# Mean squares of the attention heads: summed over the partitions by GpSimd in place of TensorE

## The chip, the core and the metric

The kernel runs on one core of a Trainium2 chip. A core has a matrix engine (TensorE, PE in the profile; its weight loads are PEld), three engines that work on 128 partitions side by side (VectorE or DVE, ScalarE or ACT, GpSimd or POOL), queues that issue transfers (SP and ACT here), an on-chip memory of 128 partitions (SBUF) and accumulators for TensorE (PSUM, in banks of 512 float32 columns). Each engine takes its instructions in order, and engines wait for one another on semaphores. The metric is the device time of one execution in microseconds.

## What is computed

A block of two layers over 272 tokens (16 learned ones and 256 of input), width 1024. Each layer has a mixer of three branches (retention with 4 heads, a gated recurrence with 8, differential attention with 8) and a feed-forward part with a short convolution. What matters here: each head's output is divided by its own root mean square.

```python
def _rms(x):
    xf = x.astype(F32)
    return xf * lax.rsqrt(jnp.mean(xf * xf, axis=-1, keepdims=True) + EPS)
...
    o = _rms(from_chunks(o)) * jax.nn.silu(gate)                          # retention, 256 values a head
...
    o = _rms(from_chunks(o)) * jax.nn.silu(gate)                          # gated recurrence, 128 values a head
...
    o = _rms(o) * subln_g.astype(F32) * (1.0 - lambda_init)               # differential attention, 128 values a head
```

## The kernel before

Activations are held transposed: features on the 128 partitions, the tokens (272, in the second layer 258) along the free dimension. A mean over a head's 128 values is thus a sum over partitions.

The main work is products of weights with activations. To keep float32 precision each operand is split into a rounded high part and a low rest, and each 128x128 weight tile is used by three matmuls (`products`, lines 915 to 917: high by high, high by low, low by high). Weights come from HBM in chunks of eight tiles, 512 KB (`_Weights.next`): a transfer to `wraw` (three buffers), ScalarE rounds it to `whi`, VectorE subtracts to `wlo` (four buffers each). The order of the products is written out in `ORDER`; a name with `+` there starts a job that runs behind the products: `hg_heads`, `hg_outputs` (gated recurrence, four heads at a time), `ret_head` (retention), `da_heads` (differential attention, two heads at a time), `da_tail` (the tokens that do not fill a block).

No engine's order is written by hand. Every operation is recorded with a cost, a due time (`plan.key`) and the tiles that it touches; `_Plan.order` then runs a list schedule and fixes the order in which all engines get their instructions. A cost is a fixed part plus a part per column (`_Engine.__getattr__`, line 571 on; for GpSimd's arithmetic 0.04 us + (0.85e-3 + 1.6e-3) us per column). A handoff to another engine is booked at 0.4 us (`CROSS`), a buffer's return at 0.5 us (`FREE`). As all helpers record through one line, most instructions bear L593 in the profile, so they are told apart by their tiles.

A head's end, before the change: its output `o` (tiles `ro`, `ho`, `do`) lies in a PSUM bank of the pool "acc", which has two. `mean` squares the upper and the lower 64 partitions on ScalarE into `hsq` and `hso`, adds them on VectorE, rounds the sum on ScalarE into the upper half of `hsh`, puts the rest beside it on VectorE, and TensorE sums the 128 rows of `hsh` with a matrix of 1/128 into a PSUM bank `ms`, so that every partition holds the mean. `rsqrt` takes Ln and Exp of it on ScalarE (`hr`), and VectorE multiplies `o` by `hr`. For retention the squares of the head's two halves have been added before, and `mean` gets them as they are. `da_tail` calls it (through `sub_norm`) once for a group of four heads, with 128 columns. The norm over a token's 1024 features (`Norm.finish`) uses `mean` as well, three times; its scaled activations `y` are made on GpSimd.

Of the kernel before, what the change touches and what calls it, by code (L numbers as in the profile page):

```python
# [12 lines left out]
F32R = mybir.dt.float32r  # L13
U8 = mybir.dt.uint8
AF = mybir.ActivationFunctionType
# [4 lines left out]
P = 128  # L20
# [3 lines left out]
T = META + SEQ  # L24
D = 1024
# [532 lines left out]
class _Engine:  # L558
# [5 lines left out]
    def __getattr__(self, method):  # L564
        f = getattr(self.engine, method)

        def call(*args, **kw):
            aps = [(k, x) for k, x in list(enumerate(args)) + list(kw.items()) if isinstance(x, bass.AP)]
            outs = [x for k, x in aps if k in (0, "out", "accum_out")]
            ins = [x for k, x in aps if k not in (0, "out", "accum_out")]  # L570
            n = math.prod(outs[0].shape[1:])
            cost = self.fixed + self.each * n
            if self.name == "act":
                cost += 0.093 * (len(aps) - 2) - (0.043 if ins[0].tensor.name in self.plan.psum else 0.0)
            elif self.name == "pool" and method != "memset":
                cost += 1.6e-3 * n
            if method == "scalar_tensor_tensor":
                cost += 0.06
            if method == "reciprocal":
                cost += 7 * self.each * n  # L580
            elif method == "tensor_tensor_scan":
                cost += self.each * n
            elif method == "transpose":
                cost = 0.11
            elif method == "matmul" and args[1].dtype == F32R:
                cost = max(0.107, n / 2400 + 0.003)
            elif method == "matmul":
                cost = max(0.214 if args[1].shape[-1] > 32 else 0.07, 4 * n / 2400)
            elif method == "dma_start":
                cost = self.fixed + self.each * n * outs[0].shape[0]  # L590

            count = self.name == "pe" and (2 if method == "transpose" or args[1].dtype == F32R else 4)
            self.plan.add(self.name, lambda: f(*args, **kw), cost, outs, ins, args[2] if method == "activation" else None, count)  # L593

        return call
# [56 lines left out]
def _trace(ctx, tc, plan, a, depth, probe):  # L652
    nc = tc.nc
    act = _Engine(plan, nc.scalar, "act", 0.094, 0.833e-3)
    dve = _Engine(plan, nc.vector, "dve", 0.068, 1.042e-3)
    pe = _Engine(plan, nc.tensor, "pe", 0.0, 4 / 2400)
    pool = _Engine(plan, nc.gpsimd, "pool", 0.04, 0.85e-3)
# [7 lines left out]
    tp = ctx.enter_context(tc.tile_pool(name="tp", bufs=2))  # L665
# [6 lines left out]
    def new(pool_, shape, dt, tag, bufs, name):  # L672
        serial[0] += 1
        return plan.tile(pool_, shape, dt, tag, bufs, f"{name}_{serial[0]}")

    def fixed(shape, name, dt=F32):
        return new(cp, shape, dt, name, 1, name)
# [10 lines left out]
    def temp(cols, tag, bufs=2):  # L688
        return new(tp, [P, cols], F32, tag, bufs, tag)
# [55 lines left out]
    def ones_round(value, name):  # L745
        t = fixed([P, P], name, F32R)
        f = slot("ones")[:, :P]
        pool.memset(f, value)
        act.activation(t, f, AF.Copy)
        return t  # L750
# [8 lines left out]
    ones_h = ones_round(1.0 / 128, "ones_h")  # L759
# [11 lines left out]
    rstd = fixed([P, T], "rstd")  # L771
# [37 lines left out]
    def rsqrt(out, ms, scale=1.0):  # L809

        act.activation(out, ms, AF.Ln, bias=eps, scale=scale)
        act.activation(out, out, AF.Exp, scale=-0.5)

    class Norm:
# [34 lines left out]
        def finish(self):  # L849
            if self.rest is None:  # L850
                self.halves()
            else:
                tt(self.sum, self.sum, self.rest, ADD)
            if self.apart:
                rsqrt(rstd[:, self.first :], mean(ones_h, self.sum, AF.Copy), P / D)
            else:

                ps = bank("ms")[:, self.first : T]
                pe.matmul(ps, ones_d, self.sum, start=True, stop=True)
                rsqrt(rstd[:, self.first :], ps)  # L860
# [106 lines left out]

    top, low = slice(0, P // 2), slice(P // 2, P)

    def mean(ones_, x, func):  # L970


        n = x.shape[1]
        sums = x[top] if func == AF.Copy else temp(T, "hsq")[top, :n]
        other = temp(T, "hso", 1)[top, :n]
        act.activation(other, x[low], func)
        if func != AF.Copy:
            act.activation(sums, x[top], func)
        tt(sums, sums, other, ADD)
        both = new(tp, [P, T], F32R, "hsh", 2, "hsh")[:, :n]  # L980
        act.activation(both[top], sums, AF.Copy)
        dve.tensor_tensor(out=both[low], in0=sums, in1=both[top].bitcast(F32), op=SUB)
        ms = bank("ms")[:, :n]
        pe.matmul(ms, ones_, both, start=True, stop=True)
        return ms

    def split_blocks(name, blocks, t0):

# [8 lines left out]
    for li in range(depth):  # L997
# [4 lines left out]
        t0 = T0 if last else 0  # L1002
# [29 lines left out]
        def ret_head(hd):  # L1032
            q, k, vt, gate = st["rq"], st["rk"], st["rvt"], st["rg"]
            if hd == 0:
                st["dec"] = slot4("dec")
                sync.dma_start(st["dec"].rearrange("p h t -> p (h t)"), a["dec"])
            dec = st["dec"][:, hd, :]

            s1 = bank("s1")
            a1 = temp(T + P + TAIL, "wts")  # L1040
            parts = ((0, t0, t0, dec[:, t0:]), (P, P, T, dec[:, : P + TAIL]))
            for k0, q0, at, _ in parts:
                pe.matmul(s1[:, at : at + T - q0], k[:, hd, k0 : k0 + P], q[:, hd, q0:], start=True, stop=True)
                plan.hold(a1)
            for _, q0, at, by in parts:
                tt(a1[:, at : at + T - q0], s1[:, at : at + T - q0], by, MUL)
            os = [acc_bank("ro") for _ in range(2)]
            sq = temp2("sum", 1)
            for e in range(2):
                o = os[e]  # L1050
                ec = slice((hd * 2 + e) % 4 * P, (hd * 2 + e) % 4 * P + P)
                v = vt[(hd * 2 + e) // 4]
                pe.matmul(o[:, t0:T], v[:, 0, ec], a1[:, t0:T], start=True, stop=False)
                pe.matmul(o[:, P:T], v[:, 1, ec], a1[:, T : T + P + TAIL], start=False, stop=True)
            for e in range(2):
                i = (e * 4 + hd) * TAIL
                tt(os[e][:, 2 * P : T], os[e][:, 2 * P : T], st["ro"][:, i : i + TAIL], ADD)
            for e in range(2):
                act.activation(sq[:, e, t0:], os[e][:, t0:T], AF.Square)
            tt(sq[:, 0, t0:], sq[:, 0, t0:], sq[:, 1, t0:], ADD)  # L1060
            r = temp(T, "hr")
            rsqrt(r[:, t0:], mean(ones_h, sq[:, 0, t0:], AF.Copy), 0.5)
            for e in range(2):
                g = gate[:, hd * 2 + e, t0:]
                y = temp(T, "ho")[:, t0:]
                tt(y, os[e][:, t0:T], r[:, t0:], MUL)
                tt(g, y, g, MUL)
# [242 lines left out]
        def hg_outputs(b, am, at, ax):  # L1310
            vt = st[f"hvt{b}"]
            pt = bank("ht")[:, : 4 * TAIL]
            pe.matmul(pt, st[f"hvs{b}"], am, start=True, stop=True)
            inside = temp(4 * TAIL, "am", 3)
            act.activation(inside, pt, AF.Copy)
            for hd in range(4):
                g = st["hg"][:, 4 * b + hd, t0:]
                o = acc_bank("ho")
                ec = slice(hd * P, hd * P + P)
                pe.matmul(o[:, t0:P], vt[:, 0, ec], at[:, hd, t0:P], start=True, stop=False)  # L1320
                pe.matmul(o[:, P:T], vt[:, 0, ec], ax[:, hd, :], start=False, stop=False)
                pe.matmul(o[:, P:T], vt[:, 1, ec], at[:, hd, P:], start=False, stop=True)
                tt(o[:, 2 * P : T], o[:, 2 * P : T], inside[:, hd * TAIL : (hd + 1) * TAIL], ADD)
                r = temp(T, "hr")
                rsqrt(r[:, t0:], mean(ones_h, o[:, t0:T], AF.Square))
                y = temp(T, "ho")[:, t0:]
                tt(y, o[:, t0:T], r[:, t0:], MUL)
                tt(g, y, g, MUL)
# [97 lines left out]
        def sub_norm(out, o):  # L1426
            n = o.shape[1]
            r = temp(T, "hr")[:, :n]
            rsqrt(r, mean(ones_h, o, AF.Square))
            stt(out, o, subg[:, li : li + 1], r, MUL, MUL)  # L1430

        def da_tail(b):
# [111 lines left out]
        for name, j in ORDER:  # L1544
# [18 lines left out]
            elif name[0] == "*":  # L1563
                plan.key = clock[0] - MARGIN
                n = name[1:]
# [9 lines left out]
            both = slice(2 * j, 2 * j + 2)  # L1575
            if name in BASE:
# [32 lines left out]
                elif name in ("hi", "dv"):  # L1609
                    n = name[0] + "v"  # L1610
# [115 lines left out]
```

## Time and profile before

| | |
|---|---|
| time, median of 3 runs | 1301.69 us (1301.66 to 1302.56) |
| span of the profiled execution, first to last instruction | 1299.9 us |
| matmuls, busy | 10965, 1290.8 us |
| VectorE, busy | 993.4 us |
| ScalarE, busy | 855.9 us |
| GpSimd, busy | 85.6 us, 162 instructions |
| granted TensorE clock, mean | 0.999 |
| read from HBM | 216.19 MB |

A row of the groups gives line, engine, operation, the tile written and the tiles read, shape and count, then busy time in us and the mean in ns, then the engine's idle time just before them and who ended it. A row of the waits gives who waited for whom: total us, times, longest. A row of a tile's view gives the count and the shortest, median and longest duration in ns, then the first and last start in us and the shapes. A row of the timeline gives start and duration in us. A row of the stretches gives busy time and instruction count of each engine between two times. Records of matmuls overlap, so the time that one takes is read from the spacing of their starts, or from a stretch in which TensorE is always busy.

### The profile page before, as it was taken

What the parts mean: (1) busy time and instruction counts of PE and PEld (TensorE: products, weight loads), DVE (VectorE), ACT (ScalarE), POOL (GpSimd) and SP (SyncE); (2) the same over time, 40 slices, a digit from 0 to 9 for tenths busy, and PEclk for the clock granted to TensorE, in tenths of its full rate; (3) what the DMA queues carried; (4) which work ended last, traced back from release to release, by engine and by line L of the source; (5) the groups of instructions that cost most, each with busy time, mean ns of one, the idle gap of its engine ahead of it and who ended that gap; (6) DMA issues with size and microseconds to landing.
All of it is one profiled execution on the core that took longest, in us unless ns stands there. A gap on an engine that the chain in (4) does not pass through costs nothing.

```text
span 1299.9 us, 27225 instructions
## 1 busy us (share of the span) xinstructions
PE 1290.8 (99%) x10965; PEld 1268.7 (98%) x10965; DVE 993.4 (76%) x1745; ACT 855.9 (66%) x1490; POOL 85.6 (7%) x162
## 2 busy tenths in 40 slices
PE   9999999999999999999999999999999999999998
PEld 8999999999999999999999999999999999999986
DVE  7685888698686789886565868886997868899753
ACT  6765565766777568776456664657667876787743
POOL 5000000000100020000020000000001100200000
PEclk9999999999999999999999999999999999999999
DMA  8555444435544555555555455454444456556653
GB/s 279 195 159 155 167 149 154 146 136 158 162 143 152 180 161 184 187 173 170 178 179 181 161 171 171 146 172 140 149 161 163 146 163 197 173 186 202 201 183 109
DMA packets 60751, 219.01 MB, mean 168 GB/s; under 512 B 6864, under 2 KB 6992, under 8 KB 60624
## 3 DMA queue, kind: packets, MB, share of 16 engines
q1 hardware_dynamic: 60336, 216.74, 51.6%
q8 instruction: 86, 1.41, 0.4%
q10 hardware_dynamic: 288, 0.52, 0.1%
q14 instruction: 41, 0.34, 0.1%
HBM read 216.19 MB, written 1.05 MB: 167 GB/s over the span
## 4 chain that ended last, share of the span: by engine, by line
PE 95%; DVE 3%; DMA 1%; issue 0%; SPq 0%; POOL 0%; ACT 0%; DVEq 0%
PE main L917 28%; PE main L915 28%; PE main L916 27%; PE fo L1520 2%; PE fo L1522 2%; PE fo L1521 2%; PE ds L1383 1%; PE do L593 1%; PE ro L593 1%; PE ho L593 1%; DMA wraw<-in_w 1%; PE vt L593 1%; DVE wlo L593 1%; PE wt L593 0%; PE lev L1106 0%; PE ms L593 0%
## 5 line engine op out<-in xcount | busy, mean ns | idle before, releaser
L915 PE MATMUL main<-xh,whi 128*128 128x272 f32 (+1 forms) x2368 | 687.8, 290 | 0.7 <-ACT whi L593 0.7
L917 PE MATMUL main<-xh,wlo 128*128 128x272 f32 (+1 forms) x2368 | 679.5, 287 | 0.5 <-DVE wlo L593 0.4
L916 PE MATMUL main<-xl,whi 128*128 128x272 f32 (+1 forms) x2368 | 670.4, 283 | 0.0
L593 DVE TENSOR_TENSOR wlo<-wraw,whi 128x1024 fp32r<-128x1024 f32 (+1 forms) x408 | 496.0, 1222 | 198.7 <-ACT whi L593 195.4
L593 ACT ACTIVATE whi<-wraw 128x1024 fp32r<-128x1024 f32 (+1 forms) x408 | 426.5, 1048 | 214.0 <-PE main L916 137.5
L916 PEld LDWEIGHTS main<-xl,whi 128*128 128x128 f32 x2368 | 449.3, 190 | 0.2
L915 PEld LDWEIGHTS main<-xh,whi 128*128 128x128 f32 x2368 | 445.5, 188 | 2.1 <-ACT whi L593 0.9
L917 PEld LDWEIGHTS main<-xh,wlo 128*128 128x128 f32 x2368 | 444.6, 188 | 1.4 <-DVE wlo L593 1.4
L593 DVE SCALAR_TENSOR_TENSOR two_b<-u,small,two_b 128x256 f32<-128x256 f32 (+2 forms) x176 | 78.3, 485 | 0.7 <-ACT two_b L593 0.2
L593 POOL TENSOR_TENSOR y<-h,rstd 128x272 f32<-128x272 f32 x32 | 38.2, 1225 | 311.1 <-ACT rstd L593 311.1
L917 PE MATMUL main<-ghi,wlo 128*128 128x272 f32 x176 | 51.0, 290 | 0.0
L915 PE MATMUL main<-ghi,whi 128*128 128x272 f32 x176 | 50.8, 288 | 0.0
L916 PE MATMUL main<-glo,whi 128*128 128x272 f32 x176 | 50.2, 285 | 0.0
L593 ACT ACTIVATE two_b<-u,small 128x272 f32<-128x272 f32 (+1 forms) x88 | 49.3, 598 | 0.7 <-DVE glo L593 0.5
L593 ACT ACTIVATE u<-main 128x544 f32<-128x544 f32 (+1 forms) x40 | 24.5, 612 | 36.5 <-PE main L917 36.4
L915 PE MATMUL main<-b0hi,whi 128*128 128x272 f32 (+1 forms) x128 | 37.3, 292 | 0.0
L915 PE MATMUL main<-b1hi,whi 128*128 128x272 f32 (+1 forms) x128 | 37.3, 292 | 0.0
L917 PE MATMUL main<-yhi,wlo 128*128 128x272 f32 (+1 forms) x128 | 36.5, 286 | 0.0
L917 PE MATMUL main<-b2hi,wlo 128*128 128x272 f32 (+1 forms) x128 | 36.5, 285 | 0.0
L917 PE MATMUL main<-b0hi,wlo 128*128 128x272 f32 (+1 forms) x128 | 36.5, 285 | 0.0
L917 PE MATMUL main<-b1hi,wlo 128*128 128x272 f32 (+1 forms) x128 | 36.5, 285 | 0.0
L915 PE MATMUL main<-b2hi,whi 128*128 128x272 f32 (+1 forms) x128 | 36.4, 284 | 0.0
(268 smaller groups left out, 1951.7 us busy)
## 6 DMA issues: line engine op xcount, KB each, us to landing
wraw<-in_w SPq DMA_DIRECT2D x402, 512.0 KB, 3.6
h<-in_h SPq DMA_DIRECT2D x4, 272.0 KB, 5.3
dec<-in_dec SPq DMA_DIRECT2D x2, 544.0 KB, 4.5
wraw<-in_w SPq DMA_DIRECT2D x4, 256.0 KB, 5.0
const<-in_const SPq DMA_DIRECT2D x1, 937.0 KB, 6.8
gain<-in_gl SPq DMA_DIRECT2D x1, 512.0 KB, 5.1
out<-y ACTq DMA_DIRECT2D x2, 256.0 KB, 2.7
out<-y SPq DMA_DIRECT2D x2, 256.0 KB, 2.7
```

The lines of the kernel that those rows point to most:

```text
L593: self.plan.add(self.name, lambda: f(*args, **kw), cost, outs, ins, args[2] if method == "activation" else None, count)
L915: nc.tensor.matmul(o, wh, hi, start=first, stop=False)
L916: nc.tensor.matmul(o, wh, lo, start=False, stop=False)
L917: nc.tensor.matmul(o, wl, hi, start=False, stop=last)
L1383: nc.tensor.matmul(ss[m][:, at : at + nk], q[half, hd, q0 : q0 + P], k[half, hd, :nk], start=True, stop=True)
L1520: nc.tensor.matmul(o, gh, wh, start=False, stop=False)
L1521: nc.tensor.matmul(o, gl, wh, start=False, stop=False)
L1522: nc.tensor.matmul(o, gh, wl, start=False, stop=end)
```

## The change

For the heads, `mean` is no longer used. A new `head_rsqrt` squares the whole output on ScalarE in one instruction (for retention the squares are there already), lets GpSimd sum over the partitions with `partition_all_reduce`, which leaves the sum on every partition, and gives this to `rsqrt` with the factor 1/128 (1/256 for retention). `mean` stays for the token norms, without its squaring branch. The buffers change with it: `hso` has two instead of one, `hsh` one instead of two. The planner gets a cost for the new operation.

```diff
+            elif method == "partition_all_reduce":
+                cost = 0.4 + 5.4e-3 * n
...
-                rsqrt(rstd[:, self.first :], mean(ones_h, self.sum, AF.Copy), P / D)
+                rsqrt(rstd[:, self.first :], mean(ones_h, self.sum), P / D)
...
-    def mean(ones_, x, func):
+    def mean(ones_, x):
         n = x.shape[1]
-        sums = x[top] if func == AF.Copy else temp(T, "hsq")[top, :n]
-        other = temp(T, "hso", 1)[top, :n]
-        act.activation(other, x[low], func)
-        if func != AF.Copy:
-            act.activation(sums, x[top], func)
+        sums = x[top]
+        other = temp(T, "hso")[top, :n]
+        act.activation(other, x[low], AF.Copy)
         tt(sums, sums, other, ADD)
-        both = new(tp, [P, T], F32R, "hsh", 2, "hsh")[:, :n]
+        both = new(tp, [P, T], F32R, "hsh", 1, "hsh")[:, :n]
         act.activation(both[top], sums, AF.Copy)
         dve.tensor_tensor(out=both[low], in0=sums, in1=both[top].bitcast(F32), op=SUB)
         ms = bank("ms")[:, :n]
         pe.matmul(ms, ones_, both, start=True, stop=True)
         return ms
+
+    def head_rsqrt(r, x, func, scale=1.0):
+        n = x.shape[1]
+        sq = x
+        if func != AF.Copy:
+            sq = temp(T, "hsq")[:, :n]
+            act.activation(sq, x, func)
+        sums = temp(T, "hso")[:, :n]
+        pool.partition_all_reduce(sums, sq, channels=P, reduce_op=bass.bass_isa.ReduceOp.add)
+        rsqrt(r, sums, scale / P)
...
-            rsqrt(r[:, t0:], mean(ones_h, sq[:, 0, t0:], AF.Copy), 0.5)
+            head_rsqrt(r[:, t0:], sq[:, 0, t0:], AF.Copy, 0.5)
...
-                rsqrt(r[:, t0:], mean(ones_h, o[:, t0:T], AF.Square))
+                head_rsqrt(r[:, t0:], o[:, t0:T], AF.Square)
...
-            rsqrt(r, mean(ones_h, o, AF.Square))
+            head_rsqrt(r, o, AF.Square)
```

## The prediction

> **What bounds the kernel now.** I read the page first: busy shares, chain of waits, costliest groups.
>
> ```profile
> span 1299.9 us, 27225 instructions
> ...
> PE 1290.8 (99%) x10965; PEld 1268.7 (98%) x10965; DVE 993.4 (76%) x1745; ACT 855.9 (66%) x1490; POOL 85.6 (7%) x162
> ...
> PE 95%; DVE 3%; DMA 1%; issue 0%; SPq 0%; POOL 0%; ACT 0%; DVEq 0%
> ...
> L915 PE MATMUL main<-xh,whi 128*128 128x272 f32 (+1 forms) x2368 | 687.8, 290 | 0.7 <-ACT whi L593 0.7
> L917 PE MATMUL main<-xh,wlo 128*128 128x272 f32 (+1 forms) x2368 | 679.5, 287 | 0.5 <-DVE wlo L593 0.4
> ```
>
> TensorE is busy for 99% of the span and is 95% of the chain that ended last; before 4736 of its main products it stood idle for 1.2 us together. So a matmul less is time less, as long as nobody makes TensorE wait. Who could make it wait is in the view of waits:
>
> ```profile
> DVE wlo L593 <- ACT whi L593: 195.4, 181, 4.7
> ACT whi L593 <- PE main L916: 137.5, 109, 3.9
> ...
> ACT hr L593 <- PE ms L593: 14.8, 21, 1.4
> ```
>
> ScalarE splits weights (whi) and stood 137.5 us waiting for TensorE to give buffers back: the split runs ahead of its use, so ScalarE and VectorE may be late by some microseconds before TensorE notices. The third row is the step that is replaced.
>
> **What goes away on TensorE.** The stretches give the real price of a matmul (a record's 283 ns overlaps its neighbours):
>
> ```profile
> 420.00:475.00 55.00, 55.00 (x444) 55.00 (x443) 39.33 (x49) 32.91 (x41) 0.00 (x0) 1.00 0.54 175
> 475.00:500.00 25.00, 25.00 (x203) 25.00 (x202) 24.29 (x36) 19.36 (x33) 9.64 (x8) 1.00 0.50 158
> ...
> 1060.00:1120.00 60.00, 60.00 (x509) 60.00 (x509) 45.00 (x56) 39.52 (x52) 3.50 (x5) 1.00 0.57 184
> ```
>
> Columns: length, then busy time (count) of PE, PEld, DVE, ACT, POOL. With 272 columns a matmul takes 55.00/444 = 0.124 us (layer 0), with 258 columns 60.00/509 = 0.118 us (layer 1). The tile view of ms counts what is removed:
>
> ```profile
> L593 PE MATMUL ms<-hsh,ones_h x47: 223/283/363, 130.3 to 1115.5; 128*128 128x272 f32 x15, 128*128 128x258 f32 x12, 128*128 128x256 f32 x8, 128*128 128x242 f32 x8
> L593 ACT ACTIVATE hr<-ms,eps x44: 349/474/489, 131.6 to 1060.0; 128x272 f32<-128x272 f32 x12, 128x258 f32<-128x258 f32 x12, 128x256 f32<-128x256 f32 x8, 128x242 f32<-128x242 f32 x8
> ```
>
> 47 passes, of which 44 feed heads (44 times hr) and go; three belong to the token norms (272 columns) and stay. 12 x 0.124 + 12 x 0.118 + 8 x 0.117 + 8 x 0.110 + 4 x 0.058 (the 128-column da_tail) = 1.49 + 1.42 + 0.93 + 0.88 + 0.23 = 4.95 us, widths not measured scaled by columns.
>
> **What goes away on ScalarE and VectorE.** The tile views of hsq, hsh, hso:
>
> ```profile
> L593 DVE TENSOR_TENSOR hsq<-hsq,hso x36: 276/414/435, 126.0 to 1055.2; 64x272 f32<-64x272 f32 x8, 64x256 f32<-64x256 f32 x8, 64x258 f32<-64x258 f32 x8, 64x242 f32<-64x242 f32 x8
> L593 ACT ACTIVATE hsh<-hsq x36: 290/407/434, 127.1 to 1056.8; 64x272 fp32r<-64x272 f32 x8, 64x256 fp32r<-64x256 f32 x8, 64x258 fp32r<-64x258 f32 x8, 64x242 fp32r<-64x242 f32 x8
> L593 DVE TENSOR_TENSOR hsh<-hsq,hsh x36: 285/420/450, 128.4 to 1058.6; 64x272 fp32r<-64x272 f32 x8, 64x256 fp32r<-64x256 f32 x8, 64x258 fp32r<-64x258 f32 x8, 64x242 fp32r<-64x242 f32 x8
> L593 ACT ACTIVATE hso<-ho x16: 382/390/397, 125.1 to 934.0; 64x272 f32<-64x272 f32 x8, 64x258 f32<-64x258 f32 x8
> ```
>
> Per head VectorE loses two adds (0.41 + 0.42 us), ScalarE the rounding (0.41) and one of two half-height squares (0.39); the square left has the same columns on all 128 partitions and so about one half's time. Over 44 heads (retention drops two copies on ScalarE, same size) that is about 37 us of VectorE and 35 us of ScalarE. Neither bounds, so I book it at nothing; it pays for the contention below.
>
> **What comes in.** 44 all-reduces on GpSimd, an operation that this trace does not show. The nearest rows are GpSimd's own arithmetic at 272 columns, and a short copy:
>
> ```profile
> L593 POOL TENSOR_TENSOR y<-h,rstd x32: 778/1014/1797, 21.5 to 1125.6; 128x272 f32<-128x272 f32 x32
> ...
> L593 POOL TENSOR_TENSOR y<-h,rstd 128x272 f32<-128x272 f32 x32 | 38.2, 1225 | 311.1 <-ACT rstd L593 311.1
> L593 POOL COPY dt<-two_a 128x16 f32<-128x16 f32 x32 | 12.4, 387 | 123.1 <-DVE two_a L593 123.1
> ```
>
> Lower bound: one pass, 0.78 us. Upper bound: 128 partitions are seven doublings, seven passes of the median 1.01, so 7.1 us. I take two passes, one to gather and one to spread, 2.0 us; the planner's new price, which sets the order, says nearly the same (0.4 + 5.4e-3 x 272 = 1.87 us). The load is 44 x 2.0 = 88 us on an engine busy for 85.6 us: capacity is no issue.
>
> Is it hidden? What it replaces, in the first retention head:
>
> ```profile
> 214.92 0.43 ACT L593 ACTIVATE hso<-sum 64x272 f32<-64x272 f32 x1
> ...
> 219.25 0.49 ACT L593 ACTIVATE hr<-ms,eps 128x272 f32<-128x272 f32 x1 [1.01 <-PE ms L593]
> ...
> 221.07 0.43 DVE L593 TENSOR_TENSOR ho<-ro,hr 128x272 f32<-128x272 f32 x1
> ...
> 221.67 0.62 PE L593 MATMUL ro<-wts,rvt 128*128 128x272 f32 x2
> ```
>
> Fold, round, subtract and pass take 219.25 - 214.92 = 4.33 us with their queueing, so an all-reduce below 4 us shortens the chain to hr. Its other end is the danger: the next head's matmul starts 0.17 us after VectorE read the PSUM bank (221.07 + 0.43 = 221.50). TensorE's queue is in order, so where the planner sets that matmul too early, every main product behind it waits. It will now set it by 1.87 us. It books 0.4 us for each of three handoffs and 0.5 us for the bank, 1.7 us, where the handoff above took 0.17, so 0.7 us: margin 1.0 us, and TensorE waits only for an all-reduce beyond 1.87 + 1.0 = 2.9 us. I book no stall.
>
> On GpSimd the copies of dt, wts and tails now queue behind an all-reduce, 2 us late at most; on ScalarE Ln waits for GpSimd, with weight splits and PSUM evacuations behind it. TensorE needs these, and the lead in the second fence covers them; without it 44 late Ln by about 1 us each (the 1.4 us of the row above was the longest) would cost up to 44 us.
>
> **Contention.** VectorE's mean per group, without GpSimd at work (420 to 475 us) and during the y burst (476.9 to 486.7):
>
> ```profile
> L593 DVE TENSOR_TENSOR wlo<-wraw,whi 128x1024 fp32r<-128x1024 f32 x19 | 23.1, 1223 | 7.8 <-ACT whi L593 7.8
> ...
> L593 DVE TENSOR_TENSOR wlo<-wraw,whi 128x1024 fp32r<-128x1024 f32 x3 | 4.7, 1564 | 0.4 <-ACT whi L593 0.3
> L593 DVE SCALAR_TENSOR_TENSOR xl<-y,small,xh 128x272 fp32r<-128x272 f32 x4 | 3.4, 878 | 0.0
> ...
> L593 DVE SCALAR_TENSOR_TENSOR xl<-h,small,xh 128x272 fp32r<-128x272 f32 x8 | 3.6, 495 | 0.0
> ```
>
> During 9.6 us of GpSimd, VectorE's records grew by 3 x 0.34 + 4 x 0.38 = 2.5 us (with two u products some 3 us), a third of GpSimd's time, and TensorE stayed busy (25.00 of 25.00 in the 475 to 500 row). A third of 88 us is 30 us against the 37 removed: no net load.
>
> The Trainium skill speaks against the change here. "SBUF — State Buffer", Who interferes with whom, says that a VectorE instruction with two SBUF inputs and a GpSimd one that reads SBUF exclude each other for the whole instruction, the loser fully blocked. By that VectorE would lose all 88 us and end 51 us heavier over the 586 us of head stretches:
>
> ```profile
> sum 586.00, DVE 469.48; mean DVE 117.37
> ```
>
> That is 80% busy now and 89% by the rule. The burst bears out blocking, but not in full length, and 89% still leaves the sum as it is.
>
> **The sum.** 1299.9 - 4.95 = 1294.9 us of span. The profiled execution's span lies 1.8 us under the median of the three runs, so 1296.7 us; 0.3 us for a few late handoffs gives 1297.
>
> **Rivals.** (1) The gain is given back: the 5 us are lost where VectorE has no lead. For it: DVE is 3% of the chain, so there are places without slack, and an all-reduce ahead of a wlo there delays it by up to 2.0 us; three such places are enough in 44. Against: most splits wait on TensorE. Time: 1301 to 1302.
>
> (2) The order is wrong (the other side): GpSimd is slower than the planner prices it and TensorE waits at the next head's matmul. For it: the planner prices y at 0.04 + 2.45e-3 x 272 = 0.71 us and the row's mean is 1.225, 1.73 times as much; the all-reduce would take 1.73 x 1.87 = 3.2 us, past 2.9. At 0.34 us for each of 44 heads, 15 us, less the 5 saved: 1312. Against: not every head follows another on the same bank, and y reads two tensors from SBUF where the all-reduce reads one. It decides from 2.9 us per all-reduce.
>
> (3) The all-reduce is far slower. At 7.1 us the excess of 4.2 us over 2.9 at 44 heads is 185 us: about 1480 us. Against: nothing in the rows, only that seven full passes is the worst way to do it. "GPSIMD Engine Reference", section 3.2 of the Trainium skill, has a partition-axis tensor_reduce of [128, 2048] at 247.7 us; scaled by columns, 33 us for 272, an estimate by which the time would be beyond 2 ms. It is another instruction, and no row here shows either.
>
> **How the numbers follow.** A measurement of this kernel can tell about 0.2% (2.6 us) from no change: faster is below 1299.1, slower above 1304.3. Forecast, 0.64: 1297, own range 1294.5 to 1299.1. Given back, 0.18, all within 0.2%. Order wrong, 0.14, slower. Far slower, 0.04. So faster 0.64, same 0.18, slower 0.18. Leaving out rival 3, the upper two thirds of rival 2 and a little below 1294.5 drops under 0.2: the range is 1294.5 to 1307.
>
> **What would show it.** Right: ms x3 instead of x47, hsh on the norms alone, all-reduce records near 2 us, TensorE's busy time near 1286 us with its idle time unchanged, hr waiting for GpSimd. Wrong: all-reduces over 2.9 us or long queueing before them; TensorE idle before ro, ho, do or ds released by VectorE (rival 2); TensorE idle before main released by wlo or whi (rival 1); gaps on GpSimd that no record fills.

## The result and the profile after

| | before | after |
|---|---|---|
| time, median (all runs) | 1301.9 us (1301.66 to 1302.56, 4 runs) | 1294.1 us (1293.64 to 1294.81, 4 runs) |
| span of the profiled execution | 1299.9 us | 1292.2 us |

The ratio is 0.9941, with an interval of 0.9929 to 0.9953: 7.8 us faster, where 4.7 were forecast, and 0.4 us below the range. The direction was right, and so was the term of the removed passes; another term of the sum, booked at nothing, was not nothing. The page of the changed kernel:

```profile
span 1292.2 us, 27078 instructions
...
PE 1284.3 (99%) x10921; PEld 1263.7 (98%) x10921; DVE 975.6 (75%) x1657; ACT 827.8 (64%) x1404; POOL 174.3 (13%) x206
...
PE 98%; DMA 0%; SPq 0%; DVE 0%; issue 0%; ACT 0%; DVEq 0%
...
L595 DVE TENSOR_TENSOR wlo<-wraw,whi 128x1024 fp32r<-128x1024 f32 (+1 forms) x408 | 509.4, 1254 | 200.5 <-ACT whi L595 197.2
...
L595 POOL PARTITION_ALL_REDUCE hso<-hsq x36 | 74.5, 2091 | 94.8 <-ACT hsq L595 94.6
```

TensorE lost 44 instructions (10965 to 10921) and 6.5 us of busy time; the span lost 7.7. VectorE vanished from the chain that ended last (3% before). GpSimd doubled, to 174.3 us, without mattering. The tiles hso and ms:

```profile
L595 ACT ACTIVATE hr<-hso,eps x44: 387/506/526, 128.3 to 1045.9; 128x272 f32<-128x272 f32 x12, 128x258 f32<-128x258 f32 x12, 128x256 f32<-128x256 f32 x8, 128x242 f32<-128x242 f32 x8
L595 POOL PARTITION_ALL_REDUCE hso<-hsq x36: 1150/2012/2883, 125.6 to 1044.0; - x36
L595 POOL PARTITION_ALL_REDUCE hso<-sum x8: 1848/1866/1883, 212.9 to 886.2; - x8
...
  ACT hr L595: 7.2, 12
```

```profile
L595 PE MATMUL ms<-hsh,ones_h x3: 286/288/289, 470.6 to 1107.8; 128*128 128x272 f32 x3
```

An all-reduce takes 1.87 us at 258 to 272 columns in the retention heads and 2.09 in the mean of the others. ScalarE waited 7.2 us for it in all, against 14.8 us for TensorE's ms before.

Where do the other 2.6 us come from? The waits of TensorE, first before, then after (who waited for whom, us in total, times, longest):

```profile
PE warm L593 <- POOL ones_d L593: 1.0, 1, 1.0
PE main L915 <- ACT whi L593: 0.7, 1, 0.7
PE main L917 <- DVE wlo L593: 0.4, 2, 0.2
PE wt L593 <- POOL dt L593: 0.4, 1, 0.4
PE ro L593 <- DVE am L593: 0.4, 1, 0.4
PE ro L593 <- DVE wts L593: 0.2, 1, 0.2
```

```profile
PE warm L595 <- POOL ones_d L595: 1.0, 1, 1.0
PE main L917 <- ACT whi L595: 0.5, 1, 0.5
PE main L919 <- DVE wlo L595: 0.4, 2, 0.2
```

The first three stand at the start of the kernel and stay. The three others, 1.0 us by idle time, are in the midst of the layers and are gone. The view shows only what is left when the overlapping records of TensorE are taken off, so it shows too little: by the spacing of matmul starts these waits, at 203 to 210, 397 and 854 us, cost 1.7 us. Over the whole kernel the spacing accounts for the 7.7 us of span: take as a matmul's slot the median spacing among matmuls with as many columns, then the slots add up to 1272.9 us before and 1267.7 after, 5.2 less, and what TensorE lost beyond its slots fell from 19.7 to 17.2 us, 2.5 less. The stretches around the first and the last (busy time and count of PE, PEld, DVE, ACT, POOL; before, then after) show who was short there:

```profile
195.00:215.00 20.00, 19.76 (x275) 18.70 (x274) 18.28 (x38) 10.47 (x19) 1.01 (x1) 1.00 0.49 150
830.00:860.00 30.00, 29.62 (x423) 28.92 (x422) 27.93 (x63) 17.21 (x35) 1.51 (x4) 1.00 0.49 159
```

```profile
195.00:215.00 20.00, 20.00 (x281) 19.51 (x281) 17.22 (x37) 9.92 (x19) 2.89 (x2) 1.00 0.41 133
830.00:860.00 30.00, 30.00 (x372) 29.58 (x371) 25.95 (x54) 16.07 (x33) 3.15 (x4) 1.00 0.48 155
```

VectorE, 76% busy over the kernel, was busy for 91% (18.28 of 20) and 93% (27.93 of 30) there, and TensorE not always. After, it has 86% in both, and TensorE is never idle. That is a reading; whether the lighter load or the mere accident of another order did it is a question for experiments, since the planner orders everything anew after every change.

### The profile page after: what moved, and what is told of

Its sections match the earlier page's. It is cut to its first block, busy times and chain, and to the rows that moved or that the text cites. A ratio compares the mean times of both kernels' runs of the same rounds, so it can differ in the third digit from the quotient of the medians.

```text
span 1292.2 us, 27078 instructions
## 1 busy us (share of the span) xinstructions
PE 1284.3 (99%) x10921; PEld 1263.7 (98%) x10921; DVE 975.6 (75%) x1657; ACT 827.8 (64%) x1404; POOL 174.3 (13%) x206
## 4 chain that ended last, share of the span: by engine, by line
PE 98%; DMA 0%; SPq 0%; DVE 0%; issue 0%; ACT 0%; DVEq 0%
PE main L919 29%; PE main L917 29%; PE main L918 28%; PE fo L1533 2%; PE fo L1531 2%; PE fo L1532 2%; PE ds L1394 1%; PE do L595 1%; PE ro L595 1%; PE ho L595 1%; PE vt L595 1%; PE lev L1117 1%; PE wt L595 1%; DMA wraw<-in_w 0%; PE s L595 0%; PE px L595 0%
## 5 line engine op out<-in xcount | busy, mean ns | idle before, releaser
L919 PE MATMUL main<-xh,wlo 128*128 128x272 f32 (+1 forms) x2368 | 679.4, 287 | 0.5 <-DVE wlo L595 0.4
L595 DVE TENSOR_TENSOR wlo<-wraw,whi 128x1024 fp32r<-128x1024 f32 (+1 forms) x408 | 509.4, 1254 | 200.5 <-ACT whi L595 197.2
L919 PEld LDWEIGHTS main<-xh,wlo 128*128 128x128 f32 x2368 | 444.5, 188 | 1.2 <-DVE wlo L595 1.1
L595 POOL PARTITION_ALL_REDUCE hso<-hsq x36 | 74.5, 2091 | 94.8 <-ACT hsq L595 94.6
L919 PE MATMUL main<-ghi,wlo 128*128 128x272 f32 x176 | 51.0, 290 | 0.0
L595 POOL COPY tails<-vsrc 128x32 f32<-128x32 f32 x32 | 11.0, 360 | 209.2 <-ACT vsrc L595 203.0
L919 PE MATMUL main<-yhi,wlo 128*128 128x272 f32 (+1 forms) x128 | 36.5, 285 | 0.0
L919 PE MATMUL main<-b2hi,wlo 128*128 128x272 f32 (+1 forms) x128 | 36.5, 285 | 0.0
L919 PE MATMUL main<-b1hi,wlo 128*128 128x272 f32 (+1 forms) x128 | 36.5, 285 | 0.0
```

What stands on the lines that cost most here:

```text
L919: nc.tensor.matmul(o, wl, hi, start=False, stop=last)
```

## The experiments

All times are medians; "before" beside each set of runs was 1301.7 to 1301.8 us.

**What the passes are worth: put back alone (after_repeat).** In `products`, order unchanged (abridged):

```diff
+AGAIN = {"m0": 4, "dv": 2, "m1": 4, "m2": 1}
...
+                if again:            # not begun and name in AGAIN and AGAIN[name] > i
+                    nc.tensor.matmul(o, wh, hi, start=True, stop=True)
                 nc.tensor.matmul(o, wh, hi, start=first, stop=False)
```

> The changed kernel in its own order, with 44 matmuls put back on TensorE alone: the first matmul of 22 accumulations in each layer (products m0, dv, m1 and one of m2) is issued twice, the first copy closed and overwritten. No engine waits for them and nothing else moves. Theory A (the gain of 7.7 us is 5.1 us of removed passes, each worth just its slot, and 2.6 us of waits of TensorE that the old order had and the new one has not): 26 x 0.124 + 18 x 0.118 = 5.3 us come back, so 1294.1 + 5.3 = 1299.4 us. Rival C (a pass costs more than its slot, 7.7 / 44 = 0.175 us, and there is no second part): 1301.8 us.

Measured: 1299.6 us, 5.5 above the changed kernel (spans 5.4 apart), as theory A has it.

```profile
PE 1289.2 (99%) x10965; PEld 1268.6 (98%) x10965; DVE 975.2 (75%) x1657; ACT 828.7 (64%) x1404; POOL 173.9 (13%) x206
```

Here a matmul of 0.12 us that waited for nothing cost TensorE its slot and no more. Rival C falls.

**What they are worth: taken away alone (before_nopass).** In `mean`, for the heads (abridged):

```diff
-        pe.matmul(ms, ones_, both, start=True, stop=True)
+        plan.add("pe", lambda: None, max(0.107, n / 2400 + 0.003), [ms], [ones_, both], None, 2)
...
-        act.activation(out, ms, AF.Ln, bias=eps, scale=scale)
+        nc.scalar.activation(r, both.bitcast(F32), AF.Ln, bias=eps, scale=scale or 1.0)
```

> The kernel before in its own order, without the 44 passes of the heads on TensorE: the planner still books them, none is issued, and Ln reads hsh in place of the bank ms (the sum over the partitions is left out; hsh holds a sum in place of a difference so that it stays positive). ScalarE and VectorE do all that they did. Theory A: only the passes' slots go, 5.1 us, and the waits at 202 to 210, 396 and 854 us stay: 1301.9 - 5.1 = 1296.8 us. Rival C (all 7.7 us are the passes): 1294.2 us.

Measured: 1297.7 us, 4.1 less than before; the span is 4.4 less. The three waits of TensorE are all still there, and one of 0.2 us is new:

```profile
PE wt L593 <- POOL dt L593: 0.4, 1, 0.4
PE ro L593 <- DVE am L593: 0.4, 1, 0.4
PE ro L593 <- DVE wts L593: 0.2, 1, 0.2
PE wt L593 <- DVE wts L593: 0.2, 1, 0.2
```

So the passes are 4 to 5.5 us of the gain, and 1297.7 - 1294.1 = 3.6 us have another cause.

**The neighbours' load given back, behind the planner's back (after_loads).** At each all-reduce, on idle data (abridged):

```diff
         pool.partition_all_reduce(sums, sq, channels=P, reduce_op=bass.bass_isa.ReduceOp.add)
+            for i in range(2):       # issued with the all-reduce, not booked
+                nc.scalar.activation(r[top], const[low, :n], AF.Copy)
+                nc.vector.tensor_tensor(out=spare[top, :n], in0=const[top, :n], in1=const[top, T : T + n], op=ADD)
```

> The changed kernel in its own order, with the removed load given back to its neighbours: behind each of the 44 all-reduces ScalarE makes two copies of 64 partitions and VectorE two adds of 64 partitions on data that nobody reads; the planner does not know of them. Theory A: no change beyond 0.6 us, 1294 to 1294.7 us, since VectorE and ScalarE have a lead of several us over TensorE. Rival B (the 2.6 us come from the 37 us less of VectorE and 28 us less of ScalarE): the waits return, 1296 to 1297 us.

Measured: 1303.0 us, 8.9 above the changed kernel and above even the kernel before. Theory A's "no change" falls, and the time lies 6 us above rival B's range as well. The waits of TensorE name the place:

```profile
PE ds L595 <- DVE dk L595: 3.0, 2, 1.5
PE do L595 <- DVE da L595: 2.8, 2, 1.4
PE vm L595 <- POOL tails L595: 1.0, 1, 1.0
```

But the order did not know of this work, so it tells of late work, not yet of load.

**The same load, booked (after_loads_booked).** The four operations are recorded through the planner's own helpers.

```diff
+        for i in range(2):
+            act.activation(r[top], const[low, :n], AF.Copy)
+            tt(spare[top, :n], const[top, :n], const[top, T : T + n], ADD)
```

> The changed kernel with the same two copies of ScalarE and two adds of VectorE behind each all-reduce as in after_loads, but recorded with their costs, so that the planner sets its order with them. Rival B (the 2.6 us beyond the passes are the neighbours' lighter load): 1294.1 + 2.6 or more, 1296.7 to 1303 us, as in after_loads. Theory A' (the unbooked work of after_loads came where the order had no room for it; the load itself is worth nothing, and the 2.6 us are the accident of one order against another): 1293 to 1296 us.

Measured: 1297.5 us, 3.4 above the changed kernel. It lies where rival B has it. One order is no proof, so other orders of the same work were run.

**How much an order is worth (before_cross_low, before_cross_high, after_cross_low, after_cross_high).** One number of the planner, no other change:

```diff
-    CROSS = 0.4
+    CROSS = 0.35       # low; high: 0.45
```

> The kernel before with the handoff booked at 0.35 us in place of 0.4 us: the same instructions, another order of them. Theory A' (an order holds some us of waits by accident): the time moves by 1 to 3 us to either side of 1301.8 us. Rival (the order of before is as good as its work allows, and the 2.6 us are owed to the changed work): within 0.5 us.

> The kernel before with the handoff booked at 0.45 us in place of 0.4 us. As for before_cross_low: theory A' 1 to 3 us to either side of 1301.8 us, the rival within 0.5 us.

> The changed kernel with the handoff booked at 0.35 us: the same instructions in another order. Freed of the 44 passes (5.1 us), the orders with the old load of ScalarE and VectorE lie at 1296.6 (before), 1297.3 (before_cross_low), 1298.1 (before_cross_high), 1297.7 (before_nopass) and 1297.5 us (after_loads_booked). Rival B (the lighter load gives the rest): another order of the light load stays near 1294.1, 1293 to 1295.5 us. Theory A' (the changed kernel's order is a lucky one): 1296 to 1298 us.

> The changed kernel with the handoff booked at 0.45 us. As for after_cross_low: rival B 1293 to 1295.5 us, theory A' 1296 to 1298 us.

| booked handoff | before | before, less 5.1 us for the passes | after |
|---|---|---|---|
| 0.35 us | 1302.4 | 1297.3 | 1295.3 |
| 0.4 us | 1301.8 | 1296.7 | 1294.1 |
| 0.45 us | 1303.2 | 1298.1 | 1294.2 |

Both theories get a part. An order alone moved the time by 1.4 us before (1303.2 - 1301.8) and by 1.2 us after. The light load's three orders have a mean of 1294.5, and the old load's, with before_nopass and after_loads_booked, of 1297.5. A fourth order of the light load, after_double_price below, has 1296.5: with it the mean is 1295.0, and the nearest two of the sets are 0.2 us apart (1296.5 and 1296.7). So 2 to 3 us belong to the load, and an order of the light load can lose nearly all of it.

**Whose load (loads_dve, loads_act, and both in the order of 0.45 us).** after_loads_booked with one of its two lines left out. loads_dve keeps VectorE's adds:

> The changed kernel with VectorE's two adds of 64 partitions given back behind each all-reduce, booked, and nothing given back to ScalarE. Light orders of the changed kernel stand at 1294.1 to 1295.3 us, after_loads_booked (both given back) at 1297.5. If VectorE's load is what costs TensorE the 2.6 us: 1296.5 to 1298 us here and 1294 to 1295.3 in loads_act; if ScalarE's is, the other way about.

> The changed kernel with ScalarE's two copies of 64 partitions given back behind each all-reduce, booked, and nothing given back to VectorE. VectorE theory: 1294 to 1295.3 us; ScalarE theory: 1296.5 to 1298 us; both share it: near 1296 in either.

> loads_dve in another order (handoff booked at 0.45 us, as in after_cross_high, which stands at 1294.2 us). VectorE theory: 1296.5 to 1298 us; ScalarE theory: 1294 to 1295.3 us. An effect that is in one order and not in the other is the order's, not the engine's.

> loads_act in another order (handoff booked at 0.45 us). VectorE theory: 1294 to 1295.3 us; ScalarE theory: 1296.5 to 1298 us. An effect that is in one order and not in the other is the order's, not the engine's.

Measured: VectorE's load alone 1299.6 and 1298.2 us, 5.5 and 4.0 above the changed kernel in the same booked handoff; ScalarE's alone 1294.9 and 1296.3, 0.8 and 2.0 above. The pages of loads_dve and of loads_act:

```profile
PE 1287.5 (99%) x10921; PEld 1265.0 (97%) x10921; DVE 1004.1 (77%) x1745; ACT 827.4 (64%) x1404; POOL 190.9 (15%) x206
```

```profile
PE 1285.5 (99%) x10921; PEld 1264.3 (98%) x10921; DVE 974.0 (75%) x1657; ACT 866.9 (67%) x1494; POOL 175.6 (14%) x206
```

28.5 us more on VectorE (1004.1 - 975.6) cost 5.5 us, in the second order 30.3 us more cost 4.0; 39 and 32 us more on ScalarE cost 0.8 and 2.0, about the scatter between orders. The VectorE theory has the direction in both orders, but not the size: 1299.6 and 1298.2 lie above its range, and loads_act's 1296.3 in the second order lies between the two ranges. In 195 to 215 us loads_dve has VectorE at 93% and TensorE short again, and loads_act has neither:

```profile
195.00:215.00 20.00, 19.50 (x273) 18.61 (x273) 18.66 (x41) 9.37 (x18) 1.48 (x2) 1.00 0.38 114
```

```profile
195.00:215.00 20.00, 20.00 (x281) 19.51 (x281) 17.26 (x37) 11.25 (x21) 2.89 (x2) 1.00 0.42 131
```

This stretch tells load from order. In the seven profiles with VectorE's old load in the planner's order (before and its two other orders, before_nopass, after_loads_booked, loads_dve in both orders) VectorE is busy for 17.88 to 18.68 us of the 20, and TensorE for 19.36 to 19.86. In after, in its three other orders (after_cross_low, after_cross_high, after_double_price) and in loads_act in both orders VectorE has 17.15 to 17.26 us, and TensorE is busy throughout. Only after_loads, where the planner did not know of the load, has 18.04 us of VectorE and TensorE busy throughout. By the spacing of matmul starts this place is worth 0.4 us of the 2.5; for the other places no stretch tells load from order.

The sizes are another matter. The adds given back stand beside the all-reduces, and some all-reduces grew with them: in loads_dve the longest took 4.55 us, where the longest of the changed kernel took 2.88.

```profile
L595 POOL PARTITION_ALL_REDUCE hso<-hsq x36: 1072/2039/4551, 126.1 to 1046.2; - x36
```

By the spacing of matmul starts, the two longest stops of TensorE in loads_dve behind its first 30 us, of 1.0 us each at 328 and 971 us, come within 5 us of the ends of its two longest all-reduces. So some of the 4 to 5.5 us may be the price of a late all-reduce, which the kernel before cannot have. How much was not separated. That both loads together (1297.5) cost less than VectorE's alone shows as well that single sizes hold only to 1 or 2 us.

**The margin of the all-reduce (after_series, after_half_price, after_double_price).** First a second all-reduce ahead of the real one, not booked (abridged):

```diff
+            nc.gpsimd.partition_all_reduce(rest, sq, channels=P, reduce_op=bass.bass_isa.ReduceOp.add)
             nc.gpsimd.partition_all_reduce(sums, sq, channels=P, reduce_op=bass.bass_isa.ReduceOp.add)
```

> The changed kernel in its own order, with a second all-reduce of the same squares ahead of each real one, on GpSimd, its result unused; the planner still books 1.87 us for both. hr comes some 1.9 us later in every head, and GpSimd works 92 us more. The prediction's step (TensorE waits when an all-reduce takes more than 2.9 us where 1.87 is booked): about 3.9 us, so 1.0 us late at up to 44 heads, 1294 + 44 = up to 1338 us. Rival (only few heads follow another at once on the same bank, and the products between them run slower than booked, so that the margin is larger): within 3 us, 1294 to 1297 us.

Measured: 1326.9 us, 33 above the changed kernel, between the two forecasts. The groups of GpSimd and the waits of TensorE:

```profile
L999 POOL PARTITION_ALL_REDUCE hsh<-hsq x36 | 75.7, 2102 | 85.4 <-ACT hsq L595 85.2
L1000 POOL PARTITION_ALL_REDUCE hso<-hsq x36 | 74.3, 2065 | 0.0
```

```profile
PE vt L595 <- ACT vsrc L595: 5.7, 4, 1.7
PE ho L595 <- DVE ho L595: 4.3, 2, 2.7
PE ds L595 <- DVE dk L595: 4.2, 2, 2.8
PE do L595 <- DVE da L595: 2.3, 3, 1.2
```

The two take 4.17 us where 1.87 are booked, and TensorE waits both for the banks (ho, do) and for what ScalarE makes late (vsrc); that this stands behind a late Ln is a reading of the order, not of a record. By the spacing of matmul starts TensorE has 16 stops of over half a microsecond, up to 2.95 us, and not 44 of equal length. Then the same operations with another booked price:

```diff
-                cost = 0.4 + 5.4e-3 * n
+                cost = 0.2 + 2.7e-3 * n       # half; double: 0.8 + 10.8e-3 * n
```

> The changed kernel with the all-reduce booked at half its price, 0.2 + 2.7e-3 x 272 = 0.93 us, while it takes about 2.1. By the prediction's step the margin of 1.0 us over 1.87 puts the limit at 1.9 us here, so TensorE would wait 0.2 us in some heads, up to 44 x 0.2 = 9 us: 1294 to 1303 us. By the slope that after_series shows (25 us of span or more for 1.9 us more, over the whole), 0.93 us of lateness costs 10 us or more: 1304 us.

> The changed kernel with the all-reduce booked at twice its price, 3.74 us: the same instructions, the next head's matmuls set later than needed. No wait for an all-reduce is left; if the changed kernel holds no such wait either, nothing is to be won: 1293 to 1296 us, as for after_cross_low (rival B 1293 to 1295.5, theory A' 1296 to 1298 us).

Measured: 1298.8 us at half the price, 4.7 above, and 1296.5 at double, 2.4 above and 0.5 above the forecast. At half the price TensorE waits again where after_series and after_loads had it waiting:

```profile
PE do L595 <- DVE da L595: 0.8, 2, 0.6
PE ds L595 <- DVE dk L595: 0.5, 1, 0.5
PE vm L595 <- POOL tails L595: 0.4, 1, 0.4
```

Double the price gave nothing, and the other order that came of it cost 2.4 us. As much of the 4.7 us may thus be the order's.

**Further in the same direction (norms_too).** The three token norms as well:

```diff
-                rsqrt(rstd[:, self.first :], mean(ones_h, self.sum), P / D)
+                head_rsqrt(rstd[:, self.first :], self.sum, AF.Copy, P / D)
```

> The changed kernel with the three token norms' sums on GpSimd as well, by the same all-reduce. Three more passes of 0.12 us leave TensorE, and the chain from the last product to rstd loses four steps of 0.42 us and their handoffs against one all-reduce of 1.9 us; the products behind a norm wait for no rstd at first, so the chain is not on TensorE's path: 1294.1 - 0.4 = 1293.7 us, 1 us to either side by the order. A rival (rstd late, TensorE waits for the first products' PSUM): above 1296 us.

Measured: 1297.2 us, 3.1 above: the rival's time, by a mechanism that neither had. By the spacing of matmul starts TensorE lost 0.5, 1.5 and 1.6 us more than in the changed kernel in 450 to 500, 650 to 700 and 1100 to 1150 us, where the three norms stand, and in sum nothing elsewhere. GpSimd, then ScalarE, at the second layer's start:

```profile
662.95 1.96 POOL L595 PARTITION_ALL_REDUCE hso<-sum  x1 [178.94 <-DVE sum L595]
673.07 8.53 POOL L595 TENSOR_TENSOR y<-h,rstd 128x272 f32<-128x272 f32 x8 [8.15 <-issue]
```

```profile
666.86 0.43 ACT L595 ACTIVATE rstd<-rstd 128x272 f32<-128x272 f32 x1
```

rstd was there at 667.29 us (666.86 + 0.43), y began at 673.07. GpSimd had been done at 664.91 and stood for 8.15 us. In the first 2.4 of them rstd was not there yet; in the last 5.8 it waited for nothing that the view shows. The last section says what stands there.

None of the runs beats the changed kernel.

## Why the prediction was wrong, and where it was right

**The passes.** 44 for 4.95 us; putting back 5.3 us' worth cost 5.5, taking them away alone gave 4.1, and the slots add up to 5.2. Right.

**"Neither bounds, so I book it at nothing".** This is the step that failed. VectorE's share of 76% and the 137.5 us that ScalarE waits for TensorE were taken as cover for the whole kernel. They are averages: in 195 to 215 us VectorE was busy for over 90%, and there the lighter load made TensorE full in every order. The chain of waits had hinted at it (DVE 3%), and the prediction used this row for the rival that loses, not for the gain. TensorE's stops put the term at 2.5 us and the sets of orders at 2 to 3, with 1 to 2.4 us of scatter between orders; the runs with one load each point to VectorE's for most of it. The 0.3 us added for late handoffs did not come either. Which of VectorE's instructions count, and how work of one stretch comes to crowd another, was not traced further.

**The load itself.** ScalarE fell by 28.1 us (35 forecast). VectorE fell by 17.8, since its other records grew by about 37 - 18 = 19 us, of which wlo's 13.4 (496.0 to 509.4). That is 21% of GpSimd's 89 us more, where a third was forecast. The prediction's reading of the rule in the Trainium skill ("SBUF — State Buffer", Who interferes with whom) would have made it all of the 88 us.

**The price of the all-reduce.** 2.0 us from two passes of a measured row; 1.87 in the retention heads, 2.09 in the mean of the other 36. The size is right; that the operation makes two passes is shown by nothing, so the choice between one and seven passes was a lucky one, with the planner's price beside it. The partition-axis reduction of the Trainium skill ("GPSIMD Engine Reference", section 3.2), 33 us when scaled by columns, an estimate, is no guide to this instruction.

**The margin.** A limit of 2.9 us was forecast at a booked 1.87. At 4.17 us the step gives 44 x 1.27 = 56 us and 33 were measured; at half the price 44 x 0.2 = 9 and 4.7 were measured. The mechanism holds: a late all-reduce makes TensorE wait. The limit fits, but is not narrowed down: all-reduces of up to 2.88 us made no such wait in the changed kernel, 4.17 us did. The size was about twice too large, since TensorE stopped in some 16 places and not in 44, and of the 4.7 us a part may be the order's. Rival 2 did not happen because the booked price was true.

**Rivals 1 and 3** did not happen. "TensorE's idle time unchanged" was wrong: the three waits inside the layers went.

## What to carry to other kernels

Work removed from an engine that is "not the bound" can be worth something where that engine's busy share in a stretch of 20 to 30 us is near full: look at stretches before booking a zero. A high share alone proves nothing: in after_loads_booked VectorE has 27.82 of 30 us in 830 to 860, and TensorE is busy throughout. Where a planner sets the order, its price for a new operation must be true, since underbooking turns into waits on the engine whose queue is in order. Changes of the order alone moved the time by 1 to 2.4 us here; a gain of that size needs several orders before it is believed.

## What the runs showed of the hardware

In norms_too GpSimd stands idle for 7.0 to 8.2 us between an all-reduce and the tensor_tensor that follows, at each of the three norms. The other two gaps:

```profile
466.09 2.75 POOL L595 PARTITION_ALL_REDUCE hso<-sum  x1 [60.07 <-DVE sum L595]
475.81 8.21 POOL L595 TENSOR_TENSOR y<-h,rstd 128x272 f32<-128x272 f32 x8 [6.98 <-issue]
```

```profile
1104.83 2.71 POOL L595 PARTITION_ALL_REDUCE hso<-sum  x1 [55.09 <-DVE sum L595]
1114.92 8.97 POOL L595 TENSOR_TENSOR y<-h,rstd 128x272 f32<-128x272 f32 x8 [7.37 <-PE main L919]
```

rstd was there at 470.71 and at 1109.44 us, so 5.1 and 5.5 us of these gaps are left after it. The third row puts its gap down to TensorE (L919); the records below make that unlikely. In the changed kernel the same turn from the one to the other has 67 us of room, with a copy between them, and y follows rstd at once:

```profile
472.67 9.64 POOL L595 TENSOR_TENSOR y<-h,rstd 128x272 f32<-128x272 f32 x8 [66.77 <-ACT rstd L595]
```

```profile
472.15 0.43 ACT L595 ACTIVATE rstd<-rstd 128x272 f32<-128x272 f32 x1
```

The views leave out an instruction that the traces hold, MODIFY_POOL_CONFIG, always two at a time on GpSimd. In norms_too a pair stands at the end of each of the norms' three all-reduces (468.8, 664.9 and 1107.5 us) and others ahead of the next all-reduce (111.6, 484.2 and 751.3). In the changed kernel pairs stand at 405.9 and 1047.9 us, between the last all-reduce of a layer and y, and at 111.5 and 749.4, ahead of a layer's first all-reduce. The kernel before, which has no all-reduce, has only the pair at its start, which the other two have as well. No pair stands between an all-reduce and a copy or a memset, and a copy can follow at once: the changed kernel has one at 971.90 us, behind the all-reduce of 970.09 to 972.03. So the gap goes with a change of what GpSimd is set up to run.

The Trainium skill, "GPSIMD Engine Reference", section 2.1, has a load of about 6 us at the first call of a freshly loaded kernel, with no instruction in the profile, measured from MODIFY_POOL_CONFIG to that call less the wait for an event. Here it is 7.0 to 8.2 us from the pair to the first tensor_tensor, or 5.1 to 5.8 less the wait for rstd, which agrees in size. In the changed kernel y began 0.09 us after rstd, 67 us behind the pair: whatever the pair starts was over by then, and cost nothing where there was room for it.
